# Decay and rate up-projections: 64-row half products replaced by stacked 128-row products

## The chip, the cores and the metric

The kernel runs on 1 core of one Trainium2 chip. The metric is the device time of one execution in microseconds (us). In the profile TensorE is PE (its weight loads PEld), VectorE is DVE, ScalarE is ACT, GpSimd is POOL, and SyncE is SP, which only issues DMAs here.

## The reference

A decoder trunk of 2 layers on x of 512 tokens x 1024 columns, all float32. Each layer normalizes x, projects it to the columns of three parallel token mixers (RWKV-7 time mixing, chunked retention, a spatial gating unit) and to their gates, merges the three, and ends with a gated MLP with a causal convolution. The change touches the RWKV-7 branch. Two of its inputs come through a projection of low rank (64): the decay `w` and the rate `a`.

```python
r, k, v, wd, ad, gd = jnp.split(p, cuts, axis=-1)        # wd, ad: (512, 64) each
w = -jax.nn.softplus(-(w0 + jnp.tanh(wd) @ w_up)) - 0.5  # w_up: (64, 512)
decay = jnp.exp(-jnp.exp(w))
a = jax.nn.sigmoid(a0 + ad @ a_up)                       # a_up: (64, 512)
...
y = rwkv7_scan(r, decay, k, v, kk, a)
```

All products of the trunk (column counts up to 2816) are computed in float32 of nearly full precision.

## The kernel before

Everything is held transposed: the 128 partitions are columns, the free dimension is the 512 tokens. A product of nearly full precision is made of three: each operand is split into a high part (rounded to the type float32r) and a low part (the rest), and high x low, high x high and low x high are accumulated in PSUM. `split` (lines 132 to 138) makes the parts, the high one with a cast on ScalarE (line 136) and the low one with a subtraction on VectorE (line 137). `mm3` (lines 140 to 151; the matmuls' own line is 144) issues the three products.

The big weights stream in through `load` and `part` (lines 112 to 130): SP loads tiles of 128 x 512 into a ring of three, ScalarE casts (line 127), VectorE subtracts (line 128). One such tile feeds 12 products. `unit` loads ahead along a plan noted in a first pass over the program.

The mixer of a layer begins with `rwkv`. It loads both up-projection matrices as one tile `wua` of 128 rows: rows 0 to 63 are `w_up`, rows 64 to 127 are `a_up` (line 401, a DMA in ScalarE's queue), and splits it. `firstF` then computes the first projected columns (block 12 among them, which is `wd` in rows 0 to 63 and `ad` in rows 64 to 127) while the norm's row factors come about: line 220 sums on TensorE, line 222 is on VectorE, line 224 on POOL, line 229 transposes on TensorE, line 231 copies on ScalarE. `col` (lines 407 to 414) scales a finished column block and mixes it with the token before. Block 12 gets a Tanh on its upper half (line 417) and is split.

For each of four blocks of 128 columns (two heads each) `prep` makes the factors of the recurrence. It starts with the up-projections of its block, `pL` for the decay and `pA` for the rate (lines 439 to 442): 6 products of 64 rows each. Their results go to ScalarE (line 455 for `pL`, line 467 for `pA`) and on to a chain on VectorE (lines 456 to 479), up to `bk` and `ag`. Line 453 is a small product for the norms of the keys. Line 486 multiplies `bk` and `ag` chunk by chunk, lines 499 and 500 are two full products with a matrix of ones by blocks (`bonesR`), accumulated in a small PSUM tile `sm` like `pL` and `pA`.

After the four blocks `solve` (lines 632 to 689) inverts triangular matrices: a loop of 31 steps on VectorE, a transposition of its result (line 666), and then small products of 32 x 32 (line 680), which need that. TensorE has other work meanwhile: `fill` takes it from a list of gates and other projections (`fillers`).

The order on each engine is planned at build time, by a scheduler that works with a model of the engines' times. `keep_in_program_order` and the flag `pin` fix the place of some instructions; `high_priority` lets the loads and the splits of weights go ahead. Tiles of the pool `u` (31 of them) are reused, and a new tile waits until the old one is free.

Of the kernel before, what the change touches and what calls it, by code (L numbers as in the profile page):

```python
# [9 lines left out]
F32R = mybir.dt.float32r  # L10
AF = mybir.ActivationFunctionType
ALU = mybir.AluOpType
AX = mybir.AxisListType
ADD, SUB, MUL, POW, MAX = ALU.add, ALU.subtract, ALU.mult, ALU.pow, ALU.max
# [32 lines left out]
class Emit:  # L47
# [336 lines left out]
    def rwkv(self, l, nst):  # L384
        nc, V, A, a = self.nc, self.nc.vector, self.nc.scalar, self.a
        T, P = nc.tensor, nc.gpsimd
# [10 lines left out]
        nkk = self.small((128, 4), "nkk")  # L397
        V.tensor_scalar(nkk, pcol("kk", 4), -0.5, None, op0=MUL)
        n2, nw = self.small((128, 32), "n2"), self.small((128, 4, 4, 2), "nw")
        wua = self.u(n="wua")  # L400
        self.tc.keep_in_program_order(nc.scalar.dma_start(wua, a["wua"][l]))
        Wh, Wl = self.split(wua)

        ids, at = ((12, 4, 0), (3, 4)) if l else ((12, 4, 0, 8), (6, 7))
        ready = dict(zip(ids, self.firstF(l, ids, nst, at)))
# [1 line left out]
        def col(m):  # L407
            ps = ready.pop(m) if m in ready else self.colF(l, m)
            p = self.r(n="rwp")
            V.tensor_tensor(p, ps, self.rsF, op=MUL)  # L410
            t = self.r(n="rwc")
            A.activation(t, p, AF.Identity, scale=omu[:, m:m + 1])
            V.scalar_tensor_tensor(t[:, 1:], p[:, :511], self.p("mu", m), t[:, 1:], op0=MUL, op1=ADD)
            return t

        wa = col(12)
        A.activation(wa[0:64, :], wa[0:64, :], AF.Tanh)
        Xh, Xl = self.split(wa)

        GB = self.rwp.tile([128, 32, 128], F32, name=self.nm("GB"))  # L420
        F = self.rwp.tile([128, 4, 8], F32, name=self.nm("F"))
# [11 lines left out]
        def prep(m):  # L433


            k, r, v = kc[m], rc[m], Vf[m]
            ms = slice(m * 128, m * 128 + 128)
            pL, pA = self.sm(), self.sm()
            for i in range(3):
                w, x = (Wh, Wh, Wl)[i], (Xl, Xh, Xh)[i]  # L440
                for ks, o in ((slice(64, 128), pA), (slice(0, 64), pL)):
                    T.matmul(o, w[ks, ms], x[ks, :], start=i == 0, stop=i == 2)  # L442
            ag = self.rw((128, 2, 8, 128), "ag", 4)
            bk = self.rw((128, 8, 2, 64), "bk", 4)
            t1, t2, t3 = [self.rw((128, 2, 512), "cs", 3) for _ in range(3)]
            ld = t1[:, 0, :]
            cx = t1.rearrange("p a t -> p (a t)")[:, 504:1024].rearrange("p (c t) -> p c t", t=65)
            ci, tha = t2[:, 0, :], t2[:, 1, :]
            kkn = t3[:, 0, :]
            A.activation(kkn, k, AF.Square, scale=self.p("kk", m))  # L450
            pn = self.sm((128, 4, 2))
            for i in range(4):
                T.matmul(pn[:, i, :], kkn[:, i * 128:i * 128 + 128], self.c("bones2"), start=True, stop=True)  # L453
            V.tensor_scalar(nw[:, m], pn, 1e-24, None, op0=MAX)
            A.activation(ld, pL, AF.Tanh, scale=0.5, bias=haw[:, 4 + m:5 + m])
            V.tensor_scalar(ld, ld, -0.5 * EXP_HALF, -0.5 * EXP_HALF, op0=MUL, op1=ADD)
            V.tensor_tensor_scan(ci, self.rst, ld, 0.0, op0=MUL, op1=ADD)
            V.tensor_tensor(cx[:, :, 1:65], q8(ci), q8(ci)[:, :, 31:32].to_broadcast([128, 8, 64]), op=SUB)
            V.tensor_scalar(cx[:, :, 0:1], q8(ci)[:, :, 31:32], -1.0, None, op0=MUL)
            Eout = ci  # L460
            A.activation(q8(Eout), cx[:, :, 1:65], AF.Exp, scale=-1.0)
            A.activation(cx, cx, AF.Exp)
            Ein, Eex = cx[:, :, 1:65], cx[:, :, 0:64]
            f = F[:, m, 0:7]
            V.reciprocal(f, cx[:, 1:8, 0])
            V.tensor_tensor(f, f, cx[:, 0:7, 64], op=MUL)
            A.activation(tha, pA, AF.Tanh, scale=0.5, bias=haw[:, m:m + 1])
            for h in range(2):
                V.tensor_tensor(ag[hv[h], h, :, 64:128], q8(r)[hv[h]], Ein[hv[h]], op=MUL)
            for h in range(2):  # L470
                V.scalar_tensor_tensor(ag[hv[h], h, :, 0:64], q8(k)[hv[h]], self.p("kk", m)[hv[h]], Eex[hv[h]], op0=MUL, op1=MUL)
            V.scalar_tensor_tensor(kkn, tha, 1.0, k, op0=ADD, op1=MUL)
            A.activation(tha, tha, AF.Identity, scale=hka[:, m:m + 1], bias=oka[:, m:m + 1])
            for h in range(2):
                V.scalar_tensor_tensor(bk[hv[h], :, h, :], q8(kkn)[hv[h]], nkk[hv[h], m:m + 1], q8(Eout)[hv[h]], op0=MUL, op1=MUL)
            kp = k
            V.tensor_tensor(kp, k, tha, op=MUL)
            for h in range(2):
                V.tensor_tensor(bk[hv[h], :, 1 - h, :], q8(kp)[hv[h]], q8(Eout)[hv[h]], op=MUL)
            causal = lambda t: P.affine_select(t, t, [[0, 8], [1, 2], [1, 64]], ALU.is_ge, 0.0, base=-1, channel_multiplier=-1)  # L480
            for g in range(2):
                pgs = [self.sm((128, 4, 128)) for _ in range(2)]
                for j in range(4):
                    c = 4 * g + j
                    for h in range(2):
                        T.matmul(pgs[h][:, j, :], bk[hv[h], c, :, :].rearrange("p a t -> p (a t)"), ag[hv[h], h, c, :], start=True, stop=True)  # L486
                for h in range(2):
                    o = 1 - h
                    A.copy(GB[hv[h], 8 * m + 4 * g:8 * m + 4 * g + 4, :], pgs[h][hv[h]])
                    A.copy(ag[hv[o], h, 4 * g:4 * g + 4, :], pgs[h][hv[o]])  # L490
            for h in range(2):
                causal(GB[hv[h], 8 * m:8 * m + 8, :].rearrange("p c (a t) -> p c a t", a=2))
                causal(ag[hv[1 - h], h].rearrange("p c (a t) -> p c a t", a=2))
            d = bk[:, 0:7].rearrange("p c a t -> p c (a t)")
            P.tensor_tensor(d, d, f.unsqueeze(2).to_broadcast([128, 7, 128]), op=MUL)
            V.scalar_tensor_tensor(kp, r, self.p("rk", m), kp, op0=MUL, op1=MUL)
            kh, kl = self.split(kp, self.r)
            pbn = self.sm()
            T.matmul(pbn, self.bonesR, kl, start=True, stop=False)
            T.matmul(pbn, self.bonesR, kh, start=False, stop=True)  # L500
            V.tensor_tensor(kp, v, pbn, op=MUL)
            AG.append(ag); BK.append(bk); bv.append(kp)
# [39 lines left out]
        for c in range(8):  # L542
# [4 lines left out]
            w = W[c]  # L547
# [505 lines left out]
def _cols(v):  # L1053
    return v.reshape(-1, 128).T


def _layout(i):
    wall, wdn, pcols = [], [], []
    for l in range(L):
        w = i["w_in"][l]  # L1060
        b = RWC + RETC
        gate0 = b + SGC
        parts = [_chunks(w[:, :RWC])]
        for j in range(3):
            parts.append(_tblock(w[:, RWC + 512 * j:RWC + 512 * j + 512]))
        parts.append(_chunks(w[:, b:b + 512]))
        parts.append(_tblock(w[:, b + 512:b + 1024]))
        parts.append(_chunks(w[:, gate0:]))
        for j in range(3):
            parts.append(_chunks(i["w_branch"][l, j]).reshape(4, 2, 128, 512).transpose(0, 2, 1, 3).reshape(4, 128, 1024))  # L1070
        parts.append(_chunks(i["w_out"][l]))
        parts.append(_chunks(i["ffn_w_up"][l]).reshape(2, NFF, 128, 1024).transpose(1, 0, 2, 3).reshape(2 * NFF, 128, 1024))
        wall.append(np.concatenate(parts, 0))
        wdn.append(_chunks(i["ffn_w_down"][l]))
        c = {"n1": i["norm1_g"][l], "mu": i["rw_mu"][l], "kk": i["rw_k_k"][l], "ka": i["rw_k_a"][l], "a0": i["rw_a0"][l], "w0": i["rw_w0"][l],
             "rk": i["rw_r_k"][l], "lg": i["rw_lnx_g"][l], "lb": i["rw_lnx_b"][l], "n2": i["norm2_g"][l],
             "cw0": i["ffn_conv_w"][l, 0], "cw1": i["ffn_conv_w"][l, 1], "cw2": i["ffn_conv_w"][l, 2],
             "cb": i["ffn_conv_b"][l], "fg": i["final_g"], "sg": i["sg_ln_g"][l], "sb": i["sg_ln_b"][l]}
        pcols.append(np.concatenate([_cols(c[n]) for n in PC], 1))
    con, rot = _constants()  # L1080
    return {
        "xT": i["x"][0].T.reshape(8, 128, S).transpose(1, 0, 2),
        "con": con, "rot": rot,
        "wall": np.stack(wall), "wdn": np.stack(wdn), "pcols": np.stack(pcols),
        "wua": np.concatenate([i["rw_w_up"], i["rw_a_up"]], 1), "gup": i["rw_g_up"],
        "sgb": i["sg_b"].reshape(L, 512),
        "sgw": i["sg_w_s"].transpose(0, 3, 1, 2),
    }
# [26 lines left out]
```

## Time and profile before

| | |
|---|---|
| time, median of 3 runs | 1775.89 us (1774.39 to 1777.48) |
| the profiled execution's own time | 1773.46 us |
| span of its profile | 1771.4 us |
| TensorE busy | 1755.7 us, 9646 matmuls |
| VectorE busy | 1161.9 us |
| ScalarE busy | 784.6 us |
| POOL busy | 192.7 us |
| HBM read, written | 174.80 MB, 16.78 MB |

The span is one execution as the profiler recorded it, and the time of that execution is a little longer than its span. A line of the timeline gives the start, the duration, the engine, the source line, the operation, the tile written and the tiles read, the shape, and how many such instructions are merged in the line; in brackets is the idle time of the engine before it, and what ended that. "64\*128 64x512" is a matmul with 64 rows and 128 columns of weights, and 512 columns moved through. A line of the source view gives a count and the shortest, the median and the longest duration in ns, with the first and the last start in us.

### The profile page before, as it was taken

The page shows a single profiled execution, that of the slowest core. Times are in us where ns is not written, and L with a number is a line of the kernel's source. Part 1 is how long each engine was busy: PE and PEld are TensorE (multiplying, and loading weights), DVE is VectorE, ACT ScalarE, POOL GpSimd, SP SyncE. Part 2 cuts the span into 40 slices and gives each one's busy share as a digit, 9 for nine tenths or more (in the row PEclk, how much of TensorE's full clock was granted, in tenths as well). Part 3 has the DMA queues.
Part 4 walks back from the last instruction along what each step waited for, and adds up shares of the span by engine and source line. Part 5 has one row for each costly group of instructions (what it writes and reads, how often), then busy time and mean ns, then how long its engine had stood idle before and what let it go on. Part 6 is the DMA issues. An engine that isn't in the chain of part 4 may idle for free.

```text
span 1771.4 us, 25916 instructions
## 1 busy us (share of the span) xinstructions
PE 1755.7 (99%) x9646; PEld 1442.4 (81%) x9646; DVE 1161.9 (66%) x1996; ACT 784.6 (44%) x1333; POOL 192.7 (11%) x240
## 2 busy tenths in 40 slices
PE   9999999999999999999999999999999999999998
PEld 7878887888888888888887788778888888888887
DVE  6887736468767777753358876465676687777433
ACT  5564444544344444443245544445332454443321
POOL 0132012013300000000002220220132000000000
PEclk9999999999999999999999999999999999999999
DMA  4234432324542232243322343323154422221332
GB/s 168 78 95 143 131 108 74 113 71 157 170 137 96 96 101 96 71 119 111 108 94 72 115 142 119 102 78 132 54 169 151 148 97 95 96 97 64 113 96 84
DMA packets 104109, 193.27 MB, mean 109 GB/s; under 512 B 11952, under 2 KB 16304, under 8 KB 103984
## 3 DMA queue, kind: packets, MB, share of 16 engines
q1 hardware_dynamic: 89280, 159.42, 27.9%
q10 hardware_dynamic: 10224, 17.52, 2.9%
q0 software_dynamic: 4480, 14.68, 2.5%
q8 instruction: 76, 1.25, 0.3%
q14 instruction: 49, 0.40, 0.1%
HBM read 174.80 MB, written 16.78 MB: 108 GB/s over the span
## 4 chain that ended last, share of the span: by engine, by line
PE 97%; ACT 1%; issue 1%; DVE 1%; DMA 0%; POOLq 0%; POOL 0%; DVEq 0%
PE acc L144 89%; PE sm L561 1%; PE sm L486 1%; PE sm L442 1%; PE sm L568 1%; PE sm L577 0%; PE sm L591 0%; PE sm L856 0%; PE sm L772 0%; PE sm L761 0%; PE sm L453 0%; PE sm L551 0%; PE sm L687 0%; DMA x<-xT 0%; PE sm L144 0%
## 5 line engine op out<-in xcount | busy, mean ns | idle before, releaser
L144 PE MATMUL acc<-lo,sh 128*128 128x512 f32 x1056 | 414.8, 393 | 2.0 <-DVE lo L137 1.2
L144 PE MATMUL acc<-hi,sh 128*128 128x512 f32 x1056 | 413.8, 392 | 0.0
L144 PE MATMUL acc<-hi,sl 128*128 128x512 f32 x1056 | 412.1, 391 | 0.0
L127 ACT CAST sh<-wr 128x512 fp32r<-128x512 f32 x376 | 228.2, 611 | 380.6 <-PE acc L144 284.4
L128 DVE TENSOR_TENSOR sl<-wr,sh 128x512 fp32r<-128x512 f32 x376 | 257.8, 689 | 181.4 <-PE acc L144 99.8
L144 PE MATMUL acc<-lo,wh 128*128 128x512 f32 x640 | 253.3, 396 | 2.4 <-DVE rst L505 1.5
L144 PE MATMUL acc<-hi,wh 128*128 128x512 f32 x640 | 250.8, 392 | 0.0
L144 PE MATMUL acc<-hi,wl 128*128 128x512 f32 x640 | 249.8, 392 | 0.0
L144 PEld LDWEIGHTS acc<-lo,sh 128*128 128x128 f32 x1056 | 198.5, 188 | 44.3 <-issue 2.9
L127 ACT CAST wh<-wr 128x512 fp32r<-128x512 f32 x208 | 128.5, 619 | 237.1 <-PE acc L144 220.8
L144 PEld LDWEIGHTS acc<-hi,sl 128*128 128x128 f32 x1056 | 198.5, 188 | 40.9
L144 PEld LDWEIGHTS acc<-hi,sh 128*128 128x128 f32 x1056 | 198.6, 188 | 40.1
L128 DVE TENSOR_TENSOR wl<-wr,wh 128x512 fp32r<-128x512 f32 x208 | 150.7, 725 | 120.3 <-ACT wh L127 117.2
L144 PE MATMUL acc<-ah,sh 128*128 128x512 f32 (+1 forms) x748 | 219.6, 377 | 0.0
L144 PEld LDWEIGHTS acc<-ah,sh 128*128 128x128 f32 x748 | 137.8, 188 | 25.8
L144 PEld LDWEIGHTS acc<-lo,wh 128*128 128x128 f32 x640 | 120.3, 188 | 29.6 <-ACT wh L127 1.9
L144 PEld LDWEIGHTS acc<-hi,wl 128*128 128x128 f32 x640 | 120.3, 188 | 26.8 <-issue 1.1
L144 PE MATMUL acc<-ah,sl 128*128 128x512 f32 (+1 forms) x374 | 141.0, 377 | 0.0
L144 PEld LDWEIGHTS acc<-hi,wh 128*128 128x128 f32 x640 | 120.4, 188 | 25.2 <-issue 1.1
L907 DVE TENSOR_TENSOR fu<-acc,rsF 128x512 f32<-128x512 f32 x88 | 60.8, 690 | 69.4 <-PE acc L144 69.3
L909 ACT ACTIVATE cv<-fu,pc 128x512 f32<-128x512 f32 x88 | 71.8, 816 | 44.1 <-DVE fu L907 39.3
L144 PEld LDWEIGHTS acc<-ah,sl 128*128 128x128 f32 x374 | 70.4, 188 | 12.7
(277 smaller groups left out, 2169.5 us busy)
## 6 DMA issues: line engine op xcount, KB each, us to landing
wr<-wall SPq DMA_DIRECT2D x488, 256.0 KB, 2.6
wr<-wdn SPq DMA_DIRECT2D x80, 256.0 KB, 2.6
gd<-gth ACTq DMA_DIRECT2D x48, 256.0 KB, 3.2
gth<-gd POOLq DMA_DIRECT2D x48, 256.0 KB, 3.4
tab<-rot ACTq DMA_DIRECT2D x8, 256.0 KB, 3.3
xi<-xT SPq DMA_DIRECT2D x8, 256.0 KB, 3.1
wr<-wdn SPq DMA_DIRECT2D x16, 128.0 KB, 2.1
xd<-xi POOLq DMA_DIRECT2D x8, 256.0 KB, 2.7
```

The lines of the kernel that those rows point to most:

```text
L127: self.kept(self.nc.scalar.copy(hi[:, :n], raw[:, :n]))
L128: self.kept(self.nc.vector.tensor_tensor(lo[:, :n], raw[:, :n], hi[:, :n], op=SUB))
L144: i = self.nc.tensor.matmul(*x, **y)
L442: T.matmul(o, w[ks, ms], x[ks, :], start=i == 0, stop=i == 2)
L486: T.matmul(pgs[h][:, j, :], bk[hv[h], c, :, :].rearrange("p a t -> p (a t)"), ag[hv[h], h, c, :], start=True, stop=True)
L561: po(T.matmul(o[hv[h], m, :], AG[m][:, h, c, i:i + 64], w[:, m, h, :], start=m == 0, stop=i == 0, skip_group_check=True))
L568: po(T.matmul(pu[hv[h], 0, m, :], GB[:, 8 * m + c, 0:64], ub[:, m, h, :], start=m == 0, stop=True, skip_group_check=True))
L907: V.tensor_tensor(u, ps, self.rsF, op=MUL)
L909: A.activation(t, u, AF.Identity, scale=self.p("cw2", j), bias=self.p("cb", j))
```

## The change

Each up-projection matrix gets a tile of its own (`wus`), in which the 64 rows of its high part stand above the 64 rows of its low part; the host lays the matrix out twice, one copy above the other, so that a cast of all 128 rows and a subtraction on rows 64 to 127 make the tile. The activation of each (`Xs`) is written twice in the same way, above and below, and is then split. So one product of 128 rows computes high x (part of x) plus low x (part of x), and there are two for each of `pL` and `pA`: one with the low part of the activation, one with the high part. The sum then holds low x low as well, which was left out before. Per block there are 4 products of 128 rows instead of 6 of 64.

Per layer there are two DMAs of 256 KB for the weights instead of one, two casts and two subtractions on 64 rows instead of one each on 128, two Tanh on 64 rows instead of one, two copies of 64 rows on VectorE, and two splits instead of one. In the new file the lines from 443 on are counted 11 higher (486 is 497, 680 is 691); the new products are lines 452 and 453.

```diff
@@ rwkv
-        wua = self.u(n="wua")
-        self.tc.keep_in_program_order(nc.scalar.dma_start(wua, a["wua"][l]))
-        Wh, Wl = self.split(wua)
+        Ws = []
+        for i in range(2):
+            wua, s = self.u(n="wua"), self.u(dt=F32R, n="wus")
+            self.tc.keep_in_program_order(nc.scalar.dma_start(wua, a["wua"][l, i]))
+            A.copy(s, wua)
+            V.tensor_tensor(s[64:128, :], wua[64:128, :], s[64:128, :], op=SUB)
+            Ws.append(s)
...
         wa = col(12)
-        A.activation(wa[0:64, :], wa[0:64, :], AF.Tanh)
-        Xh, Xl = self.split(wa)
+        Xs = []
+        for i in range(2):
+            x = self.u(n="wax")
+            for h in range(2):
+                o, s = x[64 * h:64 * h + 64, :], wa[64 * i:64 * i + 64, :]
+                if i == 0:
+                    A.activation(o, s, AF.Tanh)
+                else:
+                    V.tensor_copy(o, s)
+            Xs.append(self.split(x))
@@ prep
             pL, pA = self.sm(), self.sm()
-            for i in range(3):
-                w, x = (Wh, Wh, Wl)[i], (Xl, Xh, Xh)[i]
-                for ks, o in ((slice(64, 128), pA), (slice(0, 64), pL)):
-                    T.matmul(o, w[ks, ms], x[ks, :], start=i == 0, stop=i == 2)
+            for o, w, (xh, xl) in zip((pL, pA), Ws, Xs):
+                T.matmul(o, w[:, ms], xl, start=True, stop=False)
+                T.matmul(o, w[:, ms], xh, start=False, stop=True)
@@ host layout
-        "wua": np.concatenate([i["rw_w_up"], i["rw_a_up"]], 1), "gup": i["rw_g_up"],
+        "wua": np.stack([np.concatenate([i[n]] * 2, 1) for n in ("rw_w_up", "rw_a_up")], 1), "gup": i["rw_g_up"],
```

## The prediction

> **What bounds the kernel now.** I read the page first: the span, the busy shares, the granted clock and the chain that ended last.
>
> ```profile
> span 1771.4 us, 25916 instructions
> ...
> PE 1755.7 (99%) x9646; PEld 1442.4 (81%) x9646; DVE 1161.9 (66%) x1996; ACT 784.6 (44%) x1333; POOL 192.7 (11%) x240
> ...
> PEclk9999999999999999999999999999999999999999
> ...
> PE 97%; ACT 1%; issue 1%; DVE 1%; DMA 0%; POOLq 0%; POOL 0%; DVEq 0%
> ```
>
> TensorE is on 97% of the chain, at full clock, and idle for only 1771.4 − 1755.7 = 15.7 us. So a change is worth what it does to the spacing of TensorE's instructions, as long as no other engine comes late. The "busy" time of one matmul doesn't tell that spacing, because matmuls overlap: I take distances from start to start, in the timeline. Next I read the source view of the changed line.
>
> ```profile
> L442 PE MATMUL sm<-lo,hi x16: 492/497/502, 41.1 to 1002.3; 64*128 64x512 f32 x16
> ...
> L442 PE MATMUL sm<-hi,lo x16: 386/387/394, 41.7 to 1002.9; 64*128 64x512 f32 x16
> ```
>
> These are 48 products of 64 rows (6 for each of 4 blocks in 2 layers). A half lasts 387 to 497 ns, as long as a full product. Now the timeline of TensorE around the first of them, and then around the last.
>
> ```profile
> 40.80 0.39 PE L144 MATMUL acc<-hi,wh 128*128 128x512 f32 x1
> 41.12 0.50 PE L442 MATMUL sm<-lo,hi 64*128 64x512 f32 x2
> 41.46 0.40 PE L442 MATMUL sm<-hi,hi 64*128 64x512 f32 x2
> 41.69 0.39 PE L442 MATMUL sm<-hi,lo 64*128 64x512 f32 x2
> 42.01 0.50 PE L144 MATMUL acc<-hi,wl 128*128 128x512 f32 x1
> 42.35 0.39 PE L144 MATMUL acc<-lo,wh 128*128 128x512 f32 x1
> ```
>
> ```profile
> 1001.99 0.40 PE L144 MATMUL acc<-hi,wh 128*128 128x512 f32 x1
> 1002.32 0.50 PE L442 MATMUL sm<-lo,hi 64*128 64x512 f32 x1
> 1002.66 0.40 PE L442 MATMUL sm<-hi,hi 64*128 64x512 f32 x1
> 1002.90 0.39 PE L442 MATMUL sm<-hi,lo 64*128 64x512 f32 x1
> 1003.22 0.50 PE L144 MATMUL acc<-hi,wl 128*128 128x512 f32 x1
> 1003.56 0.95 PE L453 MATMUL sm<-con,cs 128*128 128x2 f32 x8
> ```
>
> Two things are to be seen. At 41.12 both halves of a pair (rows 0 to 63 and rows 64 to 127) start together ("x2"): six products take three places. At 1002.32 three products of one half run alone, and each takes a whole place. And in both stretches four gaps are too wide: into the 64-row products (0.32), behind the first of them (0.34), out again (0.32), and behind the first full product (0.34). For comparison, full products of a like kind, accumulated into the same small PSUM tiles:
>
> ```profile
> 65.93 0.39 PE L144 MATMUL acc<-lo,wh 128*128 128x512 f32 x1
> 66.16 0.39 PE L499 MATMUL sm<-lo,bonesR 128*128 128x512 f32 x1
> 66.38 0.39 PE L500 MATMUL sm<-hi,bonesR 128*128 128x512 f32 x1
> 66.61 0.39 PE L144 MATMUL acc<-hi,wh 128*128 128x512 f32 x1
> ```
>
> They come and go without a gap: 0.68 us over three distances, 0.227 each. So a visit to 64 rows costs 0.09 + 0.11 + 0.09 + 0.11 = 0.4 us beyond its places.
>
> **The change, part by part.**
>
> *The 64-row products go.* I take each stretch from the full product before it to the second instruction behind it, less 2 x 0.227 for the full products inside. The first gives 42.35 − 40.80 − 0.45 = 1.10 us, the last 1003.56 − 1001.99 − 0.45 = 1.12. The timeline has 14 stretches from the first to the last: nine more of three single halves (seven near 1.1, two at 1.2, with a wait), one of six at 0.98, one of two at 0.63 and one of four at 0.76. Over all 14 the sum is 14.6 us: about 39 places (9 pairs, 30 singles) x 0.227 = 8.9, and 5.7 of gaps. Gone: −14.6.
>
> *32 full products come* (4 per block), with the form of L499 and L500: 32 x 0.227 = +7.3. Their price is bounded below by 0.227; above by what a place costs in the 64-row stretches, gaps included: 14.6 / 39 = 0.375, 32 x 0.375 = 12.0, which would leave 2.6 of the gain. I take 0.227, since L499 is the same shape, type and kind of PSUM tile.
>
> [...]
>
> *The order moves.* The schedule is planned at build time, so I compared the two built instruction orders. On TensorE everything outside the decay preparation and the start of the triangular solve stands as before. One thing is new: in each layer three or four of the solve's first small products (L680) come ten full products earlier, so the visit to their 32-row shape is made twice. Two more visits, at 0.2 (the two gaps 0.09 and 0.11) to 0.4 each: I take 0.3, +0.6.
>
> *Does the chain to the solve keep up?* L680 waits in TensorE's queue, and every later product behind it, for the transposed inverse from VectorE (L666), which is at the end of a chain from the last block's L486.
>
> ```profile
> 141.98 2.06 PE L486 MATMUL sm<-ag,bk 64*128 64x128 f32 x32
> ...
> 199.44 2.21 DVE L666 STREAM_TRANSPOSE cs<-cs 128x1024 f32<-128x1024 f32 x1
> ...
> 205.85 1.20 PE L680 MATMUL sm<-cs,GB 32*32 32x32 f32 x64
> ...
> 1021.36 2.06 PE L486 MATMUL sm<-ag,bk 64*128 64x128 f32 x32
> ...
> 1079.83 2.17 DVE L666 STREAM_TRANSPOSE cs<-cs 128x1024 f32<-128x1024 f32 x1
> ...
> 1082.15 1.29 PE L680 MATMUL sm<-cs,GB 32*32 32x32 f32 x64 [0.70 <-DVE cs L666]
> ```
>
> Layer 0: the chain takes 201.65 − 141.98 = 59.7 us, its cover on TensorE 63.9, slack 4.2. Layer 1: 60.6 against 60.8 with a wait of 0.70 in it. In the new order the last L486 stands earlier: between it and L680 lie 276 full products instead of 270 in layer 0, and 278 instead of 253 in layer 1, so the slack grows by 6 x 0.227 = 1.4 to 5.6, and by 25 x 0.227 = 5.7 to about 5. The wait of 0.70 goes: −0.7. From the decay products to L486 the order leaves 66 to 78 places in place of 67 to 80, apart from the first block of each layer, where 52 to 56 are left behind the rate product and 78 to 88 behind the decay product, which starts the longer chain; 52 places are still 11.8 us.
>
> ```profile
> 83.69 1.40 DVE L479 TENSOR_TENSOR bk<-rwc,cs 64x512 f32<-64x512 f32 x2
> ...
> 87.09 1.17 PE L486 MATMUL sm<-ag,bk 64*128 64x128 f32 x16
> ```
>
> The tightest block of layer 0 had 67 places and was ready at 85.09, 2.0 us before its L486. One place less costs 0.2 of that. No stall.
>
> *The added small work.* Per layer ScalarE gets a second DMA of 256 KB to issue, two casts and a Tanh more; VectorE gets two subtractions of 64 rows in place of one of 128, one more of 128 and two copies. At the 0.62 and 0.69 of the rows below that is 1.9 us more on ScalarE and at most 2.8 on VectorE, off TensorE's path while both have idle time (44% and 66% busy above). But the second DMA stands in ScalarE's queue behind the first cast, and the second cast waits for it; behind it stand the next weight cast, then on VectorE L222, then POOL's L224, then TensorE's L229.
>
> ```profile
> 22.27 0.62 ACT L136 CAST hi<-wua 128x512 fp32r<-128x512 f32 x1 [0.41 <-DMA wua<-wua]
> ...
> 22.92 0.69 DVE L137 TENSOR_TENSOR lo<-wua,hi 128x512 fp32r<-128x512 f32 x1
> ...
> 25.53 0.62 ACT L127 CAST wh<-wr 128x512 fp32r<-128x512 f32 x1 [2.10 <-PE acc L144]
> ...
> 26.79 0.16 DVE L222 TENSOR_SCALAR ms<-sm 128x4 f32<-128x4 f32 x1
> 27.02 1.01 POOL L224 TENSOR_TENSOR rs<-ms,con 128x4 f32<-128x4 f32 x1 [25.69 <-DVE ms L222]
> ...
> 29.23 0.60 PE L229 MATMUL sm<-con,rs 128*128 128x128 f32 x4
> ```
>
> ```profile
> DMA to landing us min/median/max: 3.0/3.7/4.4
> ```
>
> Issued at 22.3 to 22.9, landed after 3.0 to 4.4: the second cast starts at 25.3 to 27.3. Add cast 0.62, weight cast 0.62, its subtraction 0.69, L222 0.16, a handover of 0.1 and POOL 1.0: 28.5 to 30.5, against 29.2 on TensorE. The stall is 0 to 1.3 us; I take 0.3, since the landing of 4.4 had a larger load of the same queue right ahead of it. In layer 1 the same path ends before L229 is due. +0.3. The weight cast that is held up feeds a tile that TensorE reaches only two tiles (24 products, 5.4 us) later.
>
> *Sum:* −14.6 + 7.3 + 0.6 − 0.7 + 0.3 = −7.1 us. The profiled execution took 1773.46 us for a span of 1771.4; it becomes 1764.3 and 1766.4. It lies 2.4 us below the median of the three timed runs (1775.89), which becomes 1768.8.
>
> **Rivals.**
>
> *The halves ran at the same time anyway.* Then 24 places are replaced by 32, and the gaps don't matter: +8 x 0.227 = +1.8, 1777.7 us. For it: the "x2" rows. Against it: only 9 of 24 pairs are side by side. [...] Chance 3%.
>
> *The gaps don't belong to 64 rows* but to the first product of a new chain (a wait that isn't shown). Then the new products keep them: 39 − 32 = 7 places gained, 1.6, but 17 stretches instead of 14, +1.2: −0.4, 1775.5 us. For it: the halves, too, wait on events of the queue. Against it: L499 also starts a new chain, and has no gap. Chance 5%.
>
> *The solve comes late* (the slower side). The place is L680, which now has three or four of its products further ahead in TensorE's queue. Each microsecond by which the chain from L486 to L666 grows past 5.6 (layer 0) and 5 (layer 1) is a microsecond of stall with everything behind it. With both 12 us longer: −7.1 + 6.4 + 7 = +6.3, 1782.2 us. It is slower than before from about 9 us per layer on. For it: VectorE is the engine of this chain, and its order is changed. Against it: nothing was added to VectorE between L486 and L666. Chance 6%; that it grows by 7 to 10 us, and the time ends within 0.2%, another 4%.
>
> **How the numbers follow.** The forecast has 82%. Its low end is 1766: no stall at L229 and visits at 0.2 give 0.5 less, and the medians of both kernels scatter by the 1.5 us seen here (together some 2.1). Its high end is the upper price of the new products, 12.0 in place of 7.3: 1773.5; the stall of 1.3, visits at 0.4 and the scatter lie inside of that. A change under 0.2% (3.6 us) can't be told from none here. Faster: 82% and 2% of partial stalls, 0.84. Same: 3 + 5 + 2 = 0.10. Slower: 0.06.
>
> **What would show it.** Right: no gaps of 0.32 around the new products, their distances 0.23, L680 without a wait on L666, TensorE's span in the two preparation stretches shorter by 3 to 4 us each. Wrong: products that start 0.3 or more apart, or idle time of TensorE ahead of L229, L486 or L680 of over a microsecond.

## The result, and the profile after

| | before | after |
|---|---|---|
| median of 7 runs | 1774.4 us (1773.37 to 1777.48) | 1780.3 us (1777.48 to 1781.56) |
| the profiled execution, its span | 1773.46 us, 1771.4 us | 1780.77 us, 1778.8 us |

The change makes the kernel slower: ratio 1.0029, 95% interval 1.0018 to 1.0040, or 5.9 us. The page after, with the rows that answer to those of before:

```profile
span 1778.8 us, 25901 instructions
...
PE 1754.7 (99%) x9630; PEld 1444.2 (81%) x9630; DVE 1168.5 (66%) x2004; ACT 787.5 (44%) x1339; POOL 191.6 (11%) x240
...
PE 92%; DVE 4%; ACT 2%; issue 1%; DMA 0%; POOLq 0%; POOL 0%; DVEq 0%; ACTq 0%
PE acc L144 84%; PE sm L572 1%; DVE wl L128 1%; PE sm L497 1%; PE sm L579 1%; PE sm L588 0%; PE sm L602 0%; PE sm L867 0%; PE sm L783 0%; PE sm L772 0%; DVE ag L482 0%; ACT ag L501 0%; DVE cs L468 0%; DVE bk L486 0%; PE sm L562 0%
```

TensorE's busy time fell by 1.0 us, but its idle time rose from 15.7 to 1778.8 − 1754.7 = 24.1 us. In the chain VectorE has gone from 1% to 4%, and a line is there that was not: L128, the subtraction that makes the low part of a streamed weight tile (`wl`). The new products themselves, in the timeline of TensorE:

```profile
46.14 0.39 PE L144 MATMUL acc<-hi,wh 128*128 128x512 f32 x1
46.37 0.39 PE L452 MATMUL sm<-lo,wus 128*128 128x512 f32 x1
46.59 0.39 PE L453 MATMUL sm<-hi,wus 128*128 128x512 f32 x1
46.82 0.39 PE L144 MATMUL acc<-hi,wl 128*128 128x512 f32 x1
```

Three distances in 0.68 us, 0.227 each, no gaps. The view of the waits of TensorE after (total us, times, longest):

```profile
PE acc L144 <- DVE wl L128: 7.7, 5, 3.4
```

No wait on L128 stands among the listed waits of before. The windows view puts the loss into the two preparation stretches. Its rows give the window, its length, and then busy time and count for PE, PEld, DVE, ACT and POOL; first before, then after:

```profile
40.00:150.00 110.00, 110.00 (x586) 88.42 (x585) 89.03 (x146) 65.23 (x110) 27.23 (x20) 1.00 0.29 93
915.00:1025.00 110.00, 110.00 (x580) 88.00 (x579) 89.35 (x143) 63.83 (x107) 23.33 (x16) 1.00 0.28 96
```

```profile
40.00:150.00 110.00, 105.50 (x560) 86.57 (x559) 93.91 (x148) 62.85 (x107) 23.36 (x17) 0.98 0.27 91
915.00:1025.00 110.00, 105.98 (x567) 86.37 (x566) 89.45 (x144) 60.44 (x102) 22.84 (x16) 1.00 0.27 90
```

TensorE was never idle in these 220 us before. After, it is idle for 4.50 + 4.02 = 8.5 us of them. The longest of the stalls, in the timelines of TensorE and of VectorE after:

```profile
133.93 0.39 PE L144 MATMUL acc<-hi,wh 128*128 128x512 f32 x1
137.67 0.75 PE L144 MATMUL acc<-hi,wl 128*128 128x512 f32 x1 [3.36 <-DVE wl L128]
138.22 0.63 PE L144 MATMUL acc<-lo,wh 128*128 128x512 f32 x1
138.65 0.63 PE L144 MATMUL acc<-hi,wh 128*128 128x512 f32 x1
```

```profile
130.41 0.69 DVE L128 TENSOR_TENSOR wl<-wr,wh 128x512 fp32r<-128x512 f32 x1
131.13 0.51 DVE L532 RECIPROCAL n<-nw 64x16 f32<-64x16 f32 x2
131.67 1.51 DVE L486 SCALAR_TENSOR_TENSOR bk<-cs,nkk,cs 64x512 f32<-64x512 f32 x2
133.22 0.21 DVE L667 STREAM_TRANSPOSE TMP<-n 128x32 f32<-128x32 f32 x1
133.35 0.16 DVE L476 RECIPROCAL F<-cs 128x7 f32<-128x7 f32 x1
133.43 1.34 DVE L480 TENSOR_TENSOR ag<-rwc,cs 64x512 f32<-64x512 f32 x2
134.79 1.51 DVE L482 SCALAR_TENSOR_TENSOR ag<-rwc,pc,cs 64x512 f32<-64x512 f32 x2
136.33 0.69 DVE L366 TENSOR_TENSOR gth<-acc,rsF 128x512 f32<-128x512 f32 x1
136.94 0.68 DVE L128 TENSOR_TENSOR wl<-wr,wh 128x512 fp32r<-128x512 f32 x1
```

VectorE is not idle there. It works off its queue, in which seven groups of the last block's preparation, of the start of the solve and of the gates stand between one `wl` and the next: 136.94 − 130.41 = 6.5 us. A weight tile lasts TensorE 12 x 0.227 = 2.7 us. The casts on ScalarE that the next two subtractions need had been over since 132.4, so it is their place in VectorE's queue that holds them up:

```profile
131.24 1.12 ACT L127 CAST wh<-wr 128x512 fp32r<-128x512 f32 x2
```

The same place before has 134.35 − 129.24 = 5.1 us between them, and TensorE didn't wait:

```profile
129.24 0.65 DVE L128 TENSOR_TENSOR wl<-wr,wh 128x512 fp32r<-128x512 f32 x1
129.81 1.50 DVE L475 SCALAR_TENSOR_TENSOR bk<-cs,nkk,cs 64x512 f32<-64x512 f32 x2
131.34 0.20 DVE L465 RECIPROCAL F<-cs 128x7 f32<-128x7 f32 x1
131.46 1.34 DVE L469 TENSOR_TENSOR ag<-rwc,cs 64x512 f32<-64x512 f32 x2
132.81 1.51 DVE L471 SCALAR_TENSOR_TENSOR ag<-rwc,pc,cs 64x512 f32<-64x512 f32 x2
134.35 0.69 DVE L128 TENSOR_TENSOR wl<-wr,wh 128x512 fp32r<-128x512 f32 x1
```

Two losses come on top, in the profiled execution. Behind the stall of 3.36 us the products run at half clock (138.65 − 138.22 = 0.43 us from start to start, above) for one stretch. And at the start the first product comes at 8.96 us instead of 7.53, behind 3.06 us of idle time, with the clock down again. In the windows view the clock is the column behind POOL:

```profile
9.00:12.00 3.00, 3.00 (x7) 2.31 (x8) 3.00 (x6) 3.00 (x7) 0.00 (x0) 0.50 0.93 350
...
137.60:141.30 3.70, 3.63 (x9) 2.87 (x10) 3.64 (x8) 1.34 (x3) 0.00 (x0) 0.54 0.70 216
```

The bookkeeping of the two spans: products −7.3; idle time in the two stretches +8.5; half clock behind the long stall about +1.7 (3.70 x (1 − 0.54), by the row above); start +2.6 (the first full product behind L220 starts at 28.98 us instead of 26.36: 1.4 are there from the first product on, the other 1.2 are put down to the half clock). That is +5.5 of the 7.4 us between the spans; 1.9 are not assigned, among them the two added visits to the solve's small products, which were forecast at 0.6.

### The profile page after: what moved, and what is told of

Read it like the earlier page. It is cut to its first block, busy times and chain, and to the rows that moved or that the text cites. A ratio compares the mean times of both kernels' runs of the same rounds, so it can differ in the third digit from the quotient of the medians.

```text
span 1778.8 us, 25901 instructions
## 1 busy us (share of the span) xinstructions
PE 1754.7 (99%) x9630; PEld 1444.2 (81%) x9630; DVE 1168.5 (66%) x2004; ACT 787.5 (44%) x1339; POOL 191.6 (11%) x240
## 4 chain that ended last, share of the span: by engine, by line
PE 92%; DVE 4%; ACT 2%; issue 1%; DMA 0%; POOLq 0%; POOL 0%; DVEq 0%; ACTq 0%
PE acc L144 84%; PE sm L572 1%; DVE wl L128 1%; PE sm L497 1%; PE sm L579 1%; PE sm L588 0%; PE sm L602 0%; PE sm L867 0%; PE sm L783 0%; PE sm L772 0%; DVE ag L482 0%; ACT ag L501 0%; DVE cs L468 0%; DVE bk L486 0%; PE sm L562 0%
## 5 line engine op out<-in xcount | busy, mean ns | idle before, releaser
L128 DVE TENSOR_TENSOR sl<-wr,sh 128x512 fp32r<-128x512 f32 x376 | 257.9, 690 | 179.4 <-PE acc L144 99.7
L128 DVE TENSOR_TENSOR wl<-wr,wh 128x512 fp32r<-128x512 f32 x208 | 153.6, 739 | 128.3 <-ACT wh L127 127.2
```

The costliest lines, as they stand in the source:

```text
L128: self.kept(self.nc.vector.tensor_tensor(lo[:, :n], raw[:, :n], hi[:, :n], op=SUB))
```

## The experiments

Two theories at first. *Order*: the products save what was predicted, and the plan that was made for the changed program loses it again, by the place of L128 in VectorE's queue. *Added work*: the added casts, subtractions, copies and DMAs make VectorE or ScalarE late in any order. All ratios are to the kernel before, run beside it on the same chip, with 95% intervals. The groups of runs below were on different chips, where the median of before was 1774.4 to 1774.9 us; across groups the ratios compare better than the times.

**VectorE's order, transplanted.** A list of the planned order of one kernel is put into the other as edges that fix the order of issue (no waits); the order of the other engines is planned around it.

```diff
             e.run()
+            if last:
+                pin_order(tc)   # each VectorE instruction behind its predecessor in the other kernel's plan
```

> The kernel before once more, unchanged, to see how its own start varies. Theory order (the loss of the change comes from the place of the weights' low parts, L128, in VectorE's queue; the later first product and the half clock at the start are chance): time ratio 1.000 within 0.001, granted clock 0.999 in some executions and 0.997 in others, because the landing of the per-layer columns (pc<-pcols, 5.82 us in the trace of before, 7.24 us in that of after) varies with the same program. Theory start (the change itself makes the start later): clock 0.999 in all executions, and no half clock near 8 to 15 us.

Measured (e1): 1775.15 us, ratio 1.0001 (0.9992 to 1.0010). The mean granted clock ran from 0.996 to 0.999 over 11 executions of the same program, and in the profiled one it was 0.53 from 9 to 12 us, so a slow start happens to the kernel before, too, as theory order expected. The load that the first product waits for (`pc`) is issued at 1.51 us in the traces of both kernels; it landed at 5.8 us in the one and at 7.2 in the other.

> The changed kernel, all of its arithmetic, but VectorE's queue in the planned order of before (the eight added small instructions at the places of those that they replace). Theory order: no wait of TensorE on L128 in the two preparation zones, so the saving of the products shows: 4 to 8 us below before, ratio 0.9955 to 0.998. Theory added work (the added casts, Tanhs, copies, subtractions and DMAs make the two engines late in any order): still 3 to 6 us above before, ratio 1.002 to 1.0035, with waits on L128 or L127 as in after.

Measured (e2): 1773.57 us, ratio 0.9993 (0.9984 to 1.0002), between what the two theories expected. With VectorE's order of before the 5.9 us lost are back, but not the saving: the time can't be told from that of before, and waits on L128 of 4.2 us are left (7.7 in after). VectorE's order is not all that differs from after: the plan made around it also has products of TensorE in other places. One of the waits left, in the timelines of VectorE and of TensorE:

```profile
134.66 1.34 DVE L480 TENSOR_TENSOR ag<-rwc,cs 64x512 f32<-64x512 f32 x2
136.01 1.51 DVE L482 SCALAR_TENSOR_TENSOR ag<-rwc,pc,cs 64x512 f32<-64x512 f32 x2
137.55 0.69 DVE L128 TENSOR_TENSOR wl<-wr,wh 128x512 fp32r<-128x512 f32 x1
```

```profile
138.30 0.50 PE L144 MATMUL acc<-hi,wl 128*128 128x512 f32 x1 [1.57 <-DVE wl L128]
```

This order was made for a TensorE with half products. With shorter products it is at its weights sooner than VectorE's queue is; this is the theory *cover* in what follows.

> The kernel before, with its half products and its one small weight tile, but VectorE's queue in the planned order of after. Theory order: TensorE waits on L128 near 85 to 135 us and near 1005 to 1015 us as in after, 6 to 12 us above before, ratio 1.0035 to 1.007. Theory added work: within 1.5 us of before, ratio 0.999 to 1.001.

Measured (e3): 1791.57 us, ratio 1.0095 (1.0081 to 1.0108). The old arithmetic with VectorE in the new order loses 16.9 us, more than was expected. In the windows of 40 to 150 and 915 to 1025 us TensorE is idle for 4.26 + 4.67 = 8.9 us, as much as in after. Of the other 8 us about 1.5 are half clock behind a stall of 2.38 us (3.40 us at a mean clock of 0.56 from 930 us on); the rest was not traced (TensorE's own order, planned around it, differs in 745 places). A change of the orders alone can cost more than the whole change did.

**The start.**

```diff
-        for i in range(6):
+        for i in range(8):      # warm-up products
```

> The changed kernel with 8 instead of 6 warm-up products ahead of the first real one (line 268); the order on every engine is otherwise that of after. If the idle of 3.06 us ahead of the first product is what halves the clock for 6.83 us after it: the idle is at most 1.7 us, the clock is 1.0 until 130 us, and the time is 1 to 1.5 us below after, ratio to before 1.002 to 1.0025. If the half clock has another cause: within 0.4 us of after, ratio 1.003, and half clock still there near 9 to 15 us.

Measured (e4): 1778.82 us, ratio 1.0020 (1.0011 to 1.0029). In its profile the idle time ahead of the first product is down to 0.75 us and the half clock near 9 us is gone (1.00 from 7 to 12 us). The median is 1.5 us below after, as the first theory expected, but the two intervals overlap.

**The place of the low parts, the cover, and the ring.** The first edit takes the run e2 and moves 59 subtractions L128 ahead in VectorE's queue, such as this one:

```diff
 L476
+L128
 L480
 L480
 L482
 L482
-L128
```

The second, also from e2, doubles the new products:

```diff
-                T.matmul(o, w[:, ms], xl, start=True, stop=False)
-                T.matmul(o, w[:, ms], xh, start=False, stop=True)
+                for i in range(2):
+                    T.matmul(o, w[:, ms], xl, start=True, stop=False)
+                    T.matmul(o, w[:, ms], xh, start=False, stop=True)
```

The third and fourth deepen the ring of after and of before:

```diff
-NU, NR, NFP = 31, 16, 39
+NU, NR, NFP = 29, 16, 39
-AHEAD = {None: 2, ...}
+AHEAD = {None: 3, ...}
-            hi, lo = [self.wp.tile(..., tag=t, bufs=3) for t in ("wh", "wl")]
+            hi, lo = [self.wp.tile(..., tag=t, bufs=4) for t in ("wh", "wl")]
```

> The run of the changed kernel with VectorE's queue as before, and in addition 59 subtractions of the weights' low parts (L128) in the two preparation zones moved ahead in VectorE's queue, each to where its cast (L127) had ended in that run's trace. There TensorE waited 1.6, 1.6 and 0.7 us on L128, each time for one queued behind the pairs of L480 and L482. Theory cover (TensorE, with shorter products, reaches its weights sooner than VectorE's queue delivers them, and only the place in the queue matters): these waits go, 3 to 5 us below that run, 1768.5 to 1770.5, ratio 0.9965 to 0.998. Theory full engine (VectorE has no room left in the zones for the added work): the waits move to what was pushed back (L497, L510, L691), the time stays within 1 us of 1773.6.

Measured (e5): 1781.64 us, ratio 1.0039 (1.0026 to 1.0051): a miss for both theories. Only VectorE's queue was fixed, and the plan moved 174 instructions on ScalarE and 618 on TensorE against e2. Waits on L128 were still 4.9 us, and a new one stood at a projected column (L414), which the moved subtractions had pushed back.

```profile
PE acc L144 <- DVE wl L128: 4.9, 8, 1.5
...
PE acc L144 <- DVE rwp L414: 1.3, 1, 1.3
```

> The changed kernel with VectorE's queue as before, and each of the new products L452/L453 issued twice (the second set starts the sum anew, so that the result is the same): 32 more products by 0.227 are 7.3 us more on TensorE, about what the half products took beyond. Theory cover: TensorE is slower again, so the waits on L128 (4.2 us in the run without the doubling) shrink below 1.5, and the time rises by 2.5 to 5 us only, to 1776 to 1778.5. Theory added work (the added casts, copies and subtractions are what is late): the waits stay at about 4 us and the time rises by the whole 7.3, to 1780 to 1782.

Measured (e6): 1778.67 us, ratio 1.0021 (1.0012 to 1.0030). 7.3 us more of products cost 5.1 us, and the waits on L128 shrink from 4.2 to 1.9. That is nearer to cover than to added work, but just outside what cover expected in both (1778.5 us and 1.5). TensorE's order was planned anew here, too.

> The changed kernel, order left to the plan, with the ring of the split weights (wh, wl) four deep instead of three and three tiles prepared ahead instead of two (pool u 29 tiles instead of 31, to make room). Theories order and cover: a late L128 has one tile more of cover, 12 products by 0.227 or 2.7 us, so waits of up to 2.7 us go: 8 to 12 us below after, 1768 to 1772, ratio 0.9965 to 0.9985. If the delay isn't one of cover (the chain or pool u holds it up): within 2 us of after, ratio above 1.002.

Measured (e7): 1778.94 us, ratio 1.0025 (1.0015 to 1.0036). By its time this is the second outcome, a delay that isn't one of cover.

> The kernel before with the same ring of four and pool u of 29, as the control for the changed kernel with it. It has no wait on L128 to lose, so both theories expect it within 1.5 us of before, ratio 0.999 to 1.001; against it the changed kernel with a ring of four shows the saving of the products, 5 to 8 us.

Measured (e8): 1776.89 us, ratio 1.0016 (1.0007 to 1.0025). Both expectations were missed: the control is slower than before, and the changed kernel is 2.1 us slower than the control, where 5 to 8 us less were expected. In e7 the waits on L128 are down from 7.7 to 1.4 us, but the plan for it has 902 of VectorE's 2005 instructions elsewhere, and another wait came (`ag`, which ScalarE copies at L501):

```profile
PE sm L510 <- ACT ag L501: 4.7, 4, 1.6
...
PE acc L144 <- DVE wl L128: 1.4, 2, 0.7
```

So e5, e7 and e8 answer nothing on their own question: each came with a plan of its own. For a clean answer the orders of the other engines had to be fixed too.

**Four instructions.** The order of e2 on TensorE, VectorE and ScalarE, and four of VectorE's subtractions moved by two to four places, two of them here:

```diff
 L476
+L128
 L480
 L480
+L128
 L482
 L482
-L128
 L477
 L366
-L128
 L488
```

> The changed kernel with the order of the run with VectorE's queue as before (1773.57 us) on every engine, and four single subtractions L128 moved ahead in VectorE's queue by two to four places, from behind the pairs of L480 and L482 to before them: those for which TensorE waited there near 110, 137 and 963 us (losses 0.84, 1.73 and 1.77 us), and the one after the second. Theory cover (the saving is held up only by these few instructions' places): the three waits go, 3 to 4.5 us below that run, 1769 to 1770.6, ratio 0.9965 to 0.9978. Theory full engine (VectorE is late as a whole): TensorE waits as long a little later, within 1 us of 1773.6.

Measured (e9): 1770.2 us, ratio 0.9977 (0.9966 to 0.9987), as theory cover expected. VectorE's timeline at the place shown above, and the waits:

```profile
132.27 0.65 DVE L128 TENSOR_TENSOR wl<-wr,wh 128x512 fp32r<-128x512 f32 x1
132.83 1.38 DVE L480 TENSOR_TENSOR ag<-rwc,cs 64x512 f32<-64x512 f32 x2
134.25 0.69 DVE L128 TENSOR_TENSOR wl<-wr,wh 128x512 fp32r<-128x512 f32 x1
134.85 1.50 DVE L482 SCALAR_TENSOR_TENSOR ag<-rwc,pc,cs 64x512 f32<-64x512 f32 x2
```

```profile
PE acc L144 <- DVE wl L128: 0.8, 4, 0.3
```

The waits fall from 4.2 to 0.8 us and the time by 3.4. TensorE is idle in the two stretches for (110 − 109.74) + (110 − 109.45) = 0.8 us. VectorE as a whole had room; the changed kernel beats the one before.

**The added work by itself.**

```diff
-            for o, w, (xh, xl) in zip((pL, pA), Ws, Xs):
-                T.matmul(o, w[:, ms], xl, start=True, stop=False)
-                T.matmul(o, w[:, ms], xh, start=False, stop=True)
+            for i in range(3):
+                for ks, o, w, (xh, xl) in zip((slice(64, 128), slice(0, 64)), (pA, pL), Ws[::-1], Xs[::-1]):
+                    T.matmul(o, w[ks, ms], (xl, xh, xh)[i][ks, :], start=i == 0, stop=i == 2)
```

> All of the added work of the change (two loads, stacked weights, stacked activations, two splits) and VectorE's queue as before, but 6 half products of 64 rows per block, in the rows and the sequence of before (the low parts stand elsewhere, so the rate is left out of the sum but for its low part; shapes and counts are those of before). Against before, this is the added work alone. Theory cover: TensorE has its old time back, so no wait on L128 over 0.5 us and 1774.5 to 1776, ratio 1.000 to 1.0007. Theory added work: waits on L128 or L127 remain, 1777 or more, ratio above 1.0013.

Measured (e10): 1776.3 us, ratio 1.0009 (1.0000 to 1.0018), between what the two theories expected. The added work costs 0 to 3 us, 0.8 us of it one wait on L128 up to 963.35 us.

**The sequence of the two sums.** The diff holds a second edit that is easily passed over: the products of the rate were issued ahead of those of the decay (`pA`, `pL`), and now come behind them. These runs swap it in each kernel.

```diff
-            for o, w, (xh, xl) in zip((pL, pA), Ws, Xs):
+            for o, w, (xh, xl) in zip((pA, pL), Ws[::-1], Xs[::-1]):
```

```diff
-                for ks, o in ((slice(64, 128), pA), (slice(0, 64), pL)):
+                for ks, o in ((slice(0, 64), pL), (slice(64, 128), pA)):
```

> The changed kernel with the two products of the rate issued ahead of those of the decay, as the half products were; the plan that is made for it has 472 of VectorE's 2005 instructions in other places than after. The same arithmetic and the same instructions. Theory order: the time moves with the plan, in either direction, by more than the products' 7.3 us can explain: anywhere from 1772 to 1786, and more than 2 us from 1780. Theory added work: the same work gives the same time, within 1 us of 1780.

Measured (e11): 1772.73 us, ratio 0.9991 (0.9983 to 1.0000).

> The kernel before with the half products of the decay issued ahead of those of the rate, the sequence that the changed kernel has; the plan made for it has 353 of VectorE's 1997 instructions in other places. Theory order (a plan's luck decides several us, whichever arithmetic it is for): more than 2 us from before, most likely above it, up to 1786. Theory that the plan follows the amount of work: within 1 us of before.

Measured (e13): 1783.66 us, ratio 1.0046 (1.0033 to 1.0058). Both swaps came out as theory order expected, which left them a wide range. The waits of e13, VectorE's timeline at the longest of them, and TensorE's:

```profile
PE acc L144 <- DVE wl L128: 4.4, 5, 2.0
```

```profile
99.70 1.63 DVE L128 TENSOR_TENSOR wl<-wr,wh 128x512 fp32r<-128x512 f32 x1
101.25 0.41 DVE L456 TENSOR_SCALAR cs<-cs 128x512 f32<-128x512 f32 x1
...
109.16 1.28 DVE L128 TENSOR_TENSOR wl<-wr,wh 128x512 fp32r<-128x512 f32 x2
```

```profile
109.90 0.50 PE L144 MATMUL acc<-hi,wl 128*128 128x512 f32 x1 [2.03 <-DVE wl L128]
```

The same stall on the same line, in a kernel that has none of the change's arithmetic. The four kernels side by side:

| | rate first | decay first |
|---|---|---|
| half products | 1774.4 (before) | 1783.66, ratio 1.0046 |
| stacked products | 1772.73, ratio 0.9991 | 1780.3 (after), ratio 1.0029 |

Down a column, at one sequence, the stacked products save 1.6 and 3.0 us by the ratios, and in neither column are the intervals apart. Along a row the swap costs 8.2 and 6.7 us by the ratios (9.3 and 7.6 by the medians). It has the same sign and a like size in both kernels; whether that lies in the sequence itself or in two unlucky plans, two plans can't settle, and why the planner then puts the preparation's chain ahead of the weights' low parts was not tried.

**The two repairs together.** 

> The kernel before with 8 instead of 6 warm-up products. If the late start is chance and common to both kernels: 0.5 to 1.5 us below before, ratio 0.9991 to 0.9997, as the same edit took 1.4 us off the changed kernel. If the change itself made its start late: within 0.3 us of before or above it, since before has nothing to gain there.

Measured (e12): 1774.67 us, ratio 1.0000 (0.9991 to 1.0009). By its median this is the second outcome.

> The changed kernel with VectorE's queue as before, the four subtractions moved (1770.2 us, ratio 0.9977), and 8 instead of 6 warm-up products. If the two repairs add: 0.7 to 1.5 us below that run, 1768.7 to 1769.5, ratio 0.9968 to 0.9974. If not: 1770 and more.

Measured (e14): 1769.97 us, ratio 0.9969 (0.9956 to 0.9981), the fastest version here, but not to be told from e9 (0.9966 to 0.9987). What the warm-up is worth, and whether the change itself makes its start later, stays open: the three effects (0.0009, 0.0000 and 0.0008 in the ratio, 1.5 us at most) all lie within the intervals.

## Why the prediction was wrong

Predicted were 1768.8 us and a range to 1773.5; measured were 1780.3.

*The price of the products* held. The 32 products are 0.227 apart, without gaps; of the two ends 0.227 and 0.375 the lower one was right. That the gaps go with a new chain is refuted by the same rows. What the exchange is worth, e9 and e10 show side by side: the same added work, the same order on VectorE but for four instructions, and 0.8 and 1.0 us of waits on L128 (TensorE's order differs). The stacked products take 1770.2 us and the half products 1776.3, 6.1 us for the 14.6 − 7.3 = 7.3 of the sum. That the halves ran at the same time anyway, the first of the rivals, would have made the stacked products 1.8 us slower, and is refuted by this.

*L229 and the chain to the solve* held in after: it has no listed wait at L229, and the wait of 0.70 on the solve's transposition (L666, now L677) is gone. In layer 1 the transposition ends at 1082.10 and L691 starts at 1087.02, a slack of 4.9 us where about 5 was forecast. This hangs on the plan, too: with other plans the wait is there again, 0.7 us in e9 and 2.4 us in e11. The rival that was slower had the right engine and the wrong place.

*"The order moves"* is the step that failed. It compared the two built orders on TensorE alone, and found little. On VectorE the two orders differ in 452 of 2005 places (the added instructions put where they replace others). The next step then looked at the waits that the chain of the preparation could cause (L486, L680), and not at the other thing that stands in VectorE's queue, the low parts of the weights, which TensorE uses up at one tile in 2.7 us. Their step was missing from the sum: +8.5 us of idle time, and the half clock behind it. The sentence "off TensorE's path while both have idle time (44% and 66% busy above)" argued from a share over the whole kernel: in the stall shown, VectorE was busy for 4.03 of the 4.10 us from 133.50 to 137.60.

*The added small work*, put at nothing, measured 0 to 3 us (e10). *The swap of the two sums* was not noticed as an edit; with the plan made for it, it costs 6.7 to 8.2 us by the ratios (e11, e13), more than everything else in the diff.

With the swap undone, the change is worth −1.7 us (ratio 0.9991, an interval that reaches to 1.0000); with VectorE's order as before and four instructions in better places −4.2 (0.9977). Of the forecast's −7.1 that is short, roughly, by the added work, 1.9 by the median of e10, by the wait of 0.7 at the solve, which is there again in e9, and by the 0.8 on L128: −7.1 + 3.4 = −3.7.

## What to carry to other kernels

Where a planner orders the queues, an edit is also a new plan, so compare the planned orders on every engine, not only on the one that bounds, and look at each stream of small work that the bounding engine consumes: how long is the longest run of other instructions between two of its items, against what the engine has in hand? An experiment that changes one thing has to hold the orders of all engines, or it measures its plan. And take a diff's sequence of statements as an edit of its own: run it alone, on the kernel before.

## What the hardware showed

In after TensorE's granted clock was at half for 3.4 us behind the idle time of 3.36 us (3.70 x 2 x (1 − 0.54), by the row from 137.60 to 141.30 above), and for 6.8 us from the last 0.9 us of the idle time of 3.06 us at its start on (the clock is 0.76 from 7 to 9 us, 0.50 from 9 to 12 and 0.64 from 12 to 16). A shorter gap can do it: in e13 the idle time of 2.03 us up to 109.90 was followed, within 1 us, by half clock, most of it in this row of the windows view.

```profile
111.10:114.50 3.40, 3.40 (x10) 2.67 (x9) 3.33 (x6) 1.36 (x3) 0.00 (x0) 0.56 0.77 205
```

In e2 the idle time of 1.57 us up to 138.30 was not followed by any (the clock is 1.00 from 130 to 140 us and from 140 to 150). But the length of the gap doesn't decide it alone. In e4 an idle time of 1.89 us up to 1009.86 was followed by a clock of 0.50 from 1010.4 to 1013.8 us; in after one of 1.90 us up to 1011.78 was not (1.00 from 1011.8 to 1016), nor in e3 one of 2.20 us up to 1026.37 (1.00 from 1026.4 to 1033). In e11 an idle time of 1.19 us up to 207.54, ahead of 64 of the solve's small products, was followed by 0.50 from 209.5 to 212.9. By these rows a stall of 1.2 to 2 us can cost an estimated 1.7 us again (half of 3.4), and need not. What parts the two gaps of 1.9 us was not tested.
